# Residual and norm around a feed-forward network, token tile by token tile, and a modulation moved into a convolution

## The chip, the cores and the metric

The kernel runs on one core of a Trainium2 chip. The metric is the device time of one execution in microseconds (us). The core's engines are named as in the profile: PE (TensorE, matmuls and transposes), PEld (its weight loads), DVE (VectorE), ACT (ScalarE), POOL (GpSimd), SP (SyncE, which issues the loads).

## The reference, cut to what matters

256 tokens of width 1024 go through two layers and then a second block. Layer 0 mixes by an mLSTM and an attention, layer 1 by a convolution; each layer has a feed-forward part, dense in layer 0, a mixture of experts in layer 1. The change touches what stands around the dense one and in front of the convolution:

```python
def rmsnorm(x, g):
    xf = x.astype(F32)
    y = xf * lax.rsqrt(jnp.mean(xf * xf, axis=-1, keepdims=True) + EPS)
    return (y * g.astype(F32)).astype(x.dtype)

def adaln(cond, w, b):
    return jax.nn.silu(cond) @ w + b

def modulate(x, g, shift, scale):
    return rmsnorm(x, g) * (1 + scale) + shift

def even_layer(...):
    sh_m, sc_m, gt_m, sh_f, sc_f, gt_f = jnp.split(adaln(c, mod_w, mod_b)[:, None, :], 6, axis=-1)
...
    mix = jnp.concatenate([h_m, h_d], axis=-1) @ w_out
    x = x + gt_m * rmsnorm(mix, mix_post_g)
    y = swiglu(modulate(x, ffn_pre_g, sh_f, sc_f), ffn_w1, ffn_w3, ffn_w2)
    return x + gt_f * rmsnorm(y, ffn_post_g)

def odd_layer(...):
    sh_m, sc_m, gt_m, sh_f, sc_f, gt_f = jnp.split(adaln(c, mod_w, mod_b)[:, None, :], 6, axis=-1)
    u = modulate(x, mix_pre_g, sh_m, sc_m)
    a, g = jnp.split(u @ pw1_w + pw1_b, 2, axis=-1)
    h = a * jax.nn.sigmoid(g)
    h = depthwise_conv(h, dw_w) + dw_b
    h = jax.nn.silu(layernorm(h, ln_g, ln_b))
    y = h @ pw2_w + pw2_b
    x = x + gt_m * rmsnorm(y, mix_post_g)
...
```

`adaln` is the modulation: a vector times a 1024 x 6144 matrix. Layer 1's second and third group of 2048 columns (gate of the convolution, shift, scale and gate of the experts) are not needed before the end of the convolution.

## The kernel before, in words

The 256 tokens lie as two token tiles of 128 partitions; `X` is 128 x 2 x 1024. Matrix products are made of three products of rounded halves: `wsplit` (L247) makes of each loaded weight a high half on ACT (L257) and the rest on DVE (L258), and `mm3` issues the products (L192 to L194). The activations are split as well, into a high tile (`fuTh`, `cuTh`) and a low one (`fuTl`, `cuTl`).

Around the change the program runs so. `w_out_steps` gives the product with `w_out` in four PSUM banks (`o`, two tiles by two halves of 512 columns). `resid` (L499) takes the squares' sums of all four on ACT (`rms_rstd`, L320), makes the gated products `yg` on DVE meanwhile (L506), one root for both tiles (`rsqrt`, L286: a shift guess and three steps, each step two instructions for each column), and adds into `X` (L511). `norm_T` (L490) takes the squares of `X`, a second root, `xn` (L497), and `to_T` (L341) transposes `xn` on PE (`transpose4`, L336) and takes it out of PSUM in pieces of 128 x 256, scaled and shifted: ACT the high half (L357), DVE an unrounded copy `room` (L359) and the rest (L360). This first boundary ends with the first product of the feed-forward network, `ffn0` (L946): eleven blocks of 256 columns, in each `w1` and `w3` by `gemm_T` (`gT` is the product's bank) and then `w2` into four banks `y`. After it the same `resid` and `norm_T` make the second boundary, and the convolution `conv1` (L999) begins: 64 steps of its first matrix `pw1`, between which a depthwise convolution runs chunk by chunk, on DVE or, by shifted copies (`sh` L1044, `shs` L1047, `dw` L1053), on PE, from a padded tile `hpad` (L1024). The order of the instructions on each engine is set when the program is built, by a scheduler over the whole program; pools of PSUM banks and of slots for loads limit it.

`mod_stream` (L433) makes the modulation of a group in eight ticks: a load of 1 MB, four matmuls of 32 columns by 512 (L447; 8 records of the trace a tick), then at the eighth the bias (a DMA, L453, and an addition, L455) and a transpose into columns. In `ffn0` one tick of layer 1's groups 1 and 2 is called behind each of `w1` and `w3` (`tick=1`). `fill` draws steps of work that waits for nothing here (the memory's keys, `mem_k`, of the second block). `gate_rows` (L476) broadcasts a row of the modulation by POOL (`row_bcast`, L469) and multiplies on DVE.

Of the kernel before, what the change touches and what calls it, by code (L numbers as in the profile page):

```python
# [20 lines left out]
D = 1024  # L21
# [12 lines left out]
FILL = (3, 5, 99, 0, 8)  # L34
BEHIND = (2, 1, 4, 2)
# [122 lines left out]
class Net:  # L158
# [278 lines left out]
    def mod_stream(self, todo):  # L437


        nc, t = self.nc, self.t  # L440
        for layer, g, dst, then in todo:
            w = t[f"l{layer}_mod_w"].rearrange("(k p) n -> p k n", p=128)
            p = self.bank("mod", self.mtag)
            for k in range(KC):
                x = self.raw(w[:, k:k + 1, g * 2048:(g + 1) * 2048], 1, 2048)
                for j in range(4):
                    nc.tensor.matmul(p[32 * j:32 * j + 32, :], self.cs[:, k, :], x[:, 0, j * 512:(j + 1) * 512],  # L447
                                     start=(k == 0), stop=(k == KC - 1), tile_position=(0, 32 * j))
                if k < KC - 1:
                    yield  # L450
            b = t[f"l{layer}_mod_b"][g * 2048:(g + 1) * 2048].rearrange("(j n) -> j n", j=4)
            for r in range(2):
                nc.gpsimd.dma_start(self.modb[r:128:32, :], b)  # L453
            mrow = dst()
            nc.vector.tensor_tensor(mrow, p, self.modb, OP.add)  # L455
# [57 lines left out]

    def halved(self, x):
        return [[x[:, tt, j * 512:(j + 1) * 512] for j in range(2)] for tt in range(2)]

    def w_out_steps(self, w, mixT, half=1, bias=None):
# [4 lines left out]
        ps = [[self.bank(f"o{tt}{j}", "g") for j in range(2)] for tt in range(2)]  # L522
# [79 lines left out]
    def layer0(self):  # L602
# [3 lines left out]
        with ExitStack() as es:  # L606
# [318 lines left out]
            self.tick(99)  # L925
            w_out = self.w_out_steps(t["l0_w_out"], mixT, 0)
# [5 lines left out]
            self.resid(ys, gp, self.halved(lp0.tile([128, 2, D], F32, tag="E", name="yg", bufs=2)))  # L932
# [13 lines left out]
    def ffn0(self, gpf, m1rows):  # L946
        nc, t, tc = self.nc, self.t, self.tc
        with tc.tile_pool(name="f0", bufs=1) as fp:
            self.mods1(m1rows, fp, (1, 2))
            uT, uTp = zip(*[self.take([128, KC, 256], F32R, "fuT" + n) for n in "hl"])  # L950
            xnp = self.ring.popleft()
            self.norm_T(self.X, uT[0], uT[1], slice(0, 256), self.scale_cols(0, "fpre0", 0, 3, 4, "a_f0"), xnp)
# [3 lines left out]
            while f0 < FF:  # L956
# [11 lines left out]
                self.gemm_T(t["l0_ffn_w1"], f0, uT, 256, gate, n, "b", tick=1)  # L968
                self.gemm_T(t["l0_ffn_w3"], f0, uT, 256, up, n, "b", tick=1)
                for k2 in range(0, nb, 2):  # L970
                    kk = f0 // 128 + k2
                    w2 = self.wsplit(self.raw(w2v[:, kk:kk + 2, :], 2, D))
                    for k in range(2):
                        hi, lo = w2[k]
                        for tt in range(2):
                            ts = slice(tt * 128, (tt + 1) * 128)
                            for j in range(2):
                                js = slice(j * 512, (j + 1) * 512)
                                self.mm3(yp[tt][j], (hT[0][:, k2 + k, ts], hT[1][:, k2 + k, ts]),
                                         (hi[:, js], lo[:, js]), kk + k == 0, kk + k == FF // 128 - 1)  # L980
# [18 lines left out]
    def conv1(self, mrow):  # L999
        nc, t, tc = self.nc, self.t, self.tc  # L1000
        with tc.tile_pool(name="l1", bufs=1) as lp:
            self.mtag = "b"
            if "l0" not in self.part:
                self.mods1(mrow, lp, (0, 1, 2))
                self.tick(99)
            uT, uTp = zip(*[self.take([128, KC, 256], F32R, "cuT" + n) for n in "hl"])
            self.norm_T(self.X, uT[0], uT[1], slice(0, 256), self.scale_cols(1, "pre1", 0, 0, 1, "a_1"), lp, "sq", fill=FILL[4])
# [59 lines left out]

            for q in range(4):
# [77 lines left out]
    def moe_rows(self, mrow, sp):  # L1146
# [4 lines left out]
        sh = sp.tile([128, D], F32, name="fsh")  # L1151
        for j in range(2):
            sl = slice(j * 512, (j + 1) * 512)
            self.row_bcast(mrow[1], 2 + j, sh[:, sl])
            nc.vector.scalar_tensor_tensor(g[:, sl], self.row_bcast(mrow[2], j), 1.0, g[:, sl], op0=OP.add, op1=OP.mult)
        return g, sh
# [857 lines left out]
    def run(self):  # L2014
        nc, t, tc = self.nc, self.t, self.tc
        part = self.part
        with ExitStack() as es:
# [29 lines left out]
            with tc.tile_pool(name="l1r", bufs=1) as rp:  # L2047
# [12 lines left out]
                self.banks = {"g": 4, "b": 4}  # L2060
# [48 lines left out]
```

## Time and profile before

| | us |
|---|---|
| runs before, median of 3 | 2104.03 (2102.4 to 2105.26) |
| the profiled execution | 2107.45 |
| span of that execution in the profile | 2105.6 |
| PE busy in the span | 1954.2 (93%) |
| DVE busy | 825.5 (39%) |
| ACT busy | 574.1 (27%) |
| POOL busy | 85.8 (4%) |

The profiled execution is 3.4 us above the median; 1.85 us of it lie outside the span. [...] All times of the rows below count from the start of the span. The span covers everything; the change touches some 370 us of it, from 323 us, where the last product with `w_out` ends, to about 691 us, where the layer norm behind the convolution runs.

### The profile page before, as it was taken

Reading aid. Unit: us, or ns where it says so; the run is one execution under the profiler, and the core shown is the slowest. Engines: PE = TensorE matmul, PEld = TensorE weight load, DVE = VectorE, ACT = ScalarE, POOL = GpSimd, SP = SyncE. Lnnn points to the kernel's source line nnn. Section 1 sums busy time; section 2 is a strip of 40 time slices with the busy share of each in tenths; the row PEclk is TensorE's granted clock in tenths of the full one; section 3 lists DMA queues with packets and bytes.
Section 4 is the critical chain, followed back from the end, with each engine's and each line's share of the span. In section 5 each row is a group of like instructions: output and inputs, shape, how many; then the busy total and the mean of one; then the engine's idle time right before and its main releaser. Section 6 shows DMA issues by size and latency. Waiting matters only on the chain. (4 is left out here: it accounts for less than half of the span.)

```text
span 2105.6 us, 32429 instructions
## 1 busy us (share of the span) xinstructions
PE 1954.2 (93%) x13291; PEld 1094.8 (52%) x13291; DVE 825.5 (39%) x1721; ACT 574.1 (27%) x977; POOL 85.8 (4%) x121
## 2 busy tenths in 40 slices
PE   5999897999899899999999999998999998989996
PEld 2777665889777633333333333337733336943442
DVE  4465476444687620012101210117632225662223
ACT  3453254344433510011101101015321213421121
POOL 1010100000130000000000000002000001000000
PEclk9999898999999899999999999999999999999998
DMA  7534557875432489999999999994699998579995
GB/s 300 170 111 140 201 180 259 264 264 178 146 103 100 152 348 412 410 411 410 412 411 410 412 411 413 410 373 154 228 416 421 408 390 310 165 315 422 421 382 235
DMA packets 168659, 635.60 MB, mean 302 GB/s; under 512 B 11969, under 2 KB 57153, under 8 KB 126513
## 3 DMA queue, kind: packets, MB, share of 16 engines
q1 hardware_dynamic: 166128, 631.80, 77.8%
q8 instruction: 110, 1.80, 0.4%
q0 software_dynamic: 2080, 1.04, 0.2%
q10 hardware_dynamic: 288, 0.52, 0.1%
q14 instruction: 53, 0.43, 0.1%
HBM read 632.25 MB, written 1.05 MB: 301 GB/s over the span
## 5 line engine op out<-in xcount | busy, mean ns | idle before, releaser
L1290 PE MATMUL up<-raw,xg 128*32 128x512 f32 (+3 forms) x3456 | 393.7, 563 | 5.8 <-DMA raw<-in_l_moe_w 5.8
L258 DVE TENSOR_TENSOR wh<-raw,wh 128x1024 fp32r<-128x1024 f32 x178 | 216.9, 1224 | 192.2 <-ACT wh L257 191.7
L1290 PEld LDWEIGHTS up<-raw,xg 128*32 128x32 f32 (+1 forms) x3456 | 131.3, 114 | 253.1 <-issue 235.5
L257 ACT ACTIVATE wh<-raw 128x1024 fp32r<-128x1024 f32 x178 | 187.1, 1060 | 245.8 <-PE gT L194 87.3
L1835 PE MATMUL up<-raw,xg 128*64 128x512 f32 (+1 forms) x1088 | 211.1, 595 | 0.0
L1340 PE MATMUL y<-raw,hT 128*32 128x512 f32 (+1 forms) x1584 | 197.6, 600 | 5.0 <-DMA raw<-in_l_moe_w 5.0
L1304 DVE TENSOR_TENSOR h<-up,h 64x512 f32<-64x512 f32 (+5 forms) x63 | 40.8, 647 | 371.0 <-ACT h L1302 370.3
L1302 ACT ACTIVATE h<-up 64x512 f32<-64x512 f32 (+5 forms) x63 | 35.1, 556 | 376.9 <-PE up L1290 376.3
L1861 PE MATMUL y<-raw,hT 128*64 128x512 f32 (+1 forms) x576 | 130.6, 597 | 3.0 <-DMA raw<-in_w_down 1.8
L1835 PEld LDWEIGHTS up<-raw,xg 128*64 128x64 f32 (+1 forms) x1088 | 64.6, 127 | 123.5 <-issue 119.8
L1340 PEld LDWEIGHTS y<-raw,hT 128*32 128x32 f32 (+1 forms) x1584 | 57.2, 114 | 136.9 <-issue 118.4
L192 PE MATMUL gT<-fuTh,wh 128*128 128x256 f32 x352 | 101.0, 287 | 0.0
L193 PE MATMUL gT<-fuTl,wh 128*128 128x256 f32 x352 | 99.5, 283 | 0.0
L194 PE MATMUL gT<-fuTh,wh 128*128 128x256 f32 x352 | 99.5, 283 | 0.0
L1841 DVE TENSOR_TENSOR h<-up,h 64x512 f32<-64x512 f32 x28 | 29.6, 1056 | 154.7 <-ACT h L1840 154.5
L447 PE MATMUL mod<-raw,cs 128*32 128x512 f32 x384 | 64.0, 695 | 26.0 <-DMA raw<-in_l_mod_w 26.0
L1861 PEld LDWEIGHTS y<-raw,hT 128*64 128x64 f32 (+1 forms) x576 | 40.4, 124 | 80.6 <-issue 69.6
L192 PEld LDWEIGHTS gT<-fuTh,wh 128*128 128x128 f32 x352 | 67.4, 191 | 12.1 <-issue 10.9
L1840 ACT ACTIVATE h<-up 64x512 f32<-64x512 f32 x28 | 30.0, 1072 | 155.9 <-PE up L1835 155.9
L194 PEld LDWEIGHTS gT<-fuTh,wh 128*128 128x128 f32 x352 | 67.5, 192 | 0.3
L193 PEld LDWEIGHTS gT<-fuTl,wh 128*128 128x128 f32 x352 | 67.4, 192 | 0.2
L1870 DVE SCALAR_TENSOR_TENSOR yl<-y,gsl,yh 128x512 fp32r<-128x512 f32 x28 | 20.9, 746 | 101.4 <-ACT yh L1869 101.4
(589 smaller groups left out, 3125.3 us busy)
## 6 DMA issues: line engine op xcount, KB each, us to landing
raw<-in_l_moe_w SPq DMA_DIRECT2D x216, 1024.0 KB, 18.4
raw<-in_w_gate SPq DMA_DIRECT2D x64, 1024.0 KB, 10.6
raw<-in_w_up SPq DMA_DIRECT2D x64, 1024.0 KB, 9.7
raw<-in_w_down SPq DMA_DIRECT2D x64, 1024.0 KB, 13.0
raw<-in_l_mod_w SPq DMA_DIRECT2D x48, 1024.0 KB, 6.3
raw<-in_l_moe_w SPq DMA_DIRECT2D x64, 768.0 KB, 17.1
raw<-in_l_ffn_w SPq DMA_DIRECT2D x33, 1024.0 KB, 5.5
raw<-in_l_w_in SPq DMA_DIRECT2D x14, 1024.0 KB, 5.4
```

Of the source, the lines that this page charges most:

```text
L192: mm(out, l[0], r[0], start=start, stop=False, skip_group_check=True)
L193: mm(out, l[0], r[1], start=False, stop=False, skip_group_check=True)
L194: mm(out, l[1], r[0], start=False, stop=stop, skip_group_check=True)
L257: nc.scalar.activation(hi, x[:, k:k + s, :], AF.Copy)
L258: nc.vector.tensor_tensor(lo, x[:, k:k + s, :], hi.bitcast(F32), OP.subtract)
L447: nc.tensor.matmul(p[32 * j:32 * j + 32, :], self.cs[:, k, :], x[:, 0, j * 512:(j + 1) * 512], start=(k == 0), stop=(k == KC - 1), tile_po ...
L1290: nc.tensor.matmul(ps[b][c * t:(c + 1) * t, :hn], j.xg[:, k, s:s + t], x[w][:, k - k2, half * hn:(half + 1) * hn], start=(k == 0), stop=(k ...
L1302: nc.scalar.activation(h[a:z, js], ps[b1][o1:o1 + z - a, :hn], AF.Silu)
L1304: nc.vector.tensor_tensor(h[a:z, js], ps[b3][o3:o3 + z - a, :hn], h[a:z, js], OP.mult)
L1340: nc.tensor.matmul(j.y[b][c * t:(c + 1) * t, :], hT[:, k, s:s + t], x[:, k - k2, o * 512:(o + 1) * 512], start=(i == 0 and k == (k % 2 if ...
L1835: nc.tensor.matmul(p[o:o + t, :], xg[:, k, c:c + t], pair[w][:, k - k4, :], start=(k == 0), stop=(k == KC - 1), tile_position=(0, o))
L1861: nc.tensor.matmul(y[o][a:a + n, :], hT[:, q * m + a:q * m + a + n], x[e][:, k, o * 512:(o + 1) * 512], start=(q == 0), stop=(q == 3), til ...
```

## The change

Five things are changed.

1. `resid` and `norm_T` around the feed-forward network give way to `resid_tiles` and `norm_tiles`, which treat tile 0 and then tile 1, in an order of ACT's and DVE's instructions that is the order of the code (`ordered()`) from the first square to `xn`. Each tile has a root of its own, on operands of 128 x 1. The transposed norm leaves PSUM in pieces of 128 x 128 (16 by ACT, 16 by DVE) with four subtractions of 128 x 512, where it was 8 of 128 x 256 each by ACT, by DVE and for the subtraction.
2. In the last block of `ffn0` the products with `w2` are sorted by token tile.
3. Layer 1's groups 1 and 2 of the modulation leave `ffn0` and go into the loop over `pw1`, a tick behind every third step, in a PSUM bank of their own (tag "m"); the bias is loaded into the row itself.
4. All nine calls of `fill` come ahead of the second residual; one was there before, and eight were inside the norm.
5. The rows made of these groups: the gate behind the convolution and the shift of the experts are made behind the third quarter of the loop, the scale and the last gate behind the loop and what is left of the ticks. All were made behind the second quarter.

```diff
+    def resid_tiles(self, y, gp, yg):
...
+        for tt in range(2):
+            for j in range(2):
+                squares(sums[tt], y[tt][j], j)
+                nc.vector.tensor_tensor(yg[tt][j], y[tt][j], gp[:, j * 512:(j + 1) * 512], OP.mult)
+            r = self.rstd_of(sums[tt], D)
+            for j in range(2):
+                nc.vector.scalar_tensor_tensor(X[tt][j], yg[tt][j], r, X[tt][j], op0=OP.mult, op1=OP.add)
+                squares(sums[2 + tt], X[tt][j], j)
+        return sums[2:]
...
+    def norm_tiles(self, x, sums, hi, lo, sc, xn, chain):
+
+        nc = self.nc
+        for tt in range(2):
+            r = self.rstd_of(sums[tt], D)
+            nc.vector.tensor_scalar(xn[:, tt, :], x[:, tt, :], r, None, op0=OP.mult)
+        chain.close()
+        for k0 in (0, 4):
+            for tt in range(2):
+                ts = slice(tt * 128, (tt + 1) * 128)
+                p = self.transpose4([xn[:, tt, (k0 + i) * 128:(k0 + i + 1) * 128] for i in range(4)])
+                v = self.room()
+                for i in range(4):
+                    pv, k = p[:, i * 128:(i + 1) * 128], k0 + i
+                    nc.scalar.activation(hi[:, k, ts], pv, AF.Identity, scale=sc[0][:, k:k + 1], bias=sc[1][:, k:k + 1])
+                    nc.vector.tensor_scalar(v[:, i * 128:(i + 1) * 128], pv, sc[0][:, k:k + 1], sc[1][:, k:k + 1], op0=OP.mult, op1=OP.add)
+                nc.vector.tensor_tensor(lo[:, k0:k0 + 4, ts], v.rearrange("p (k t) -> p k t", k=4), hi[:, k0:k0 + 4, ts].bitcast(F32), OP.subtract)
...
-            self.mods1(m1rows, fp, (1, 2))
...
-                self.gemm_T(t["l0_ffn_w1"], f0, uT, 256, gate, n, "b", tick=1)
-                self.gemm_T(t["l0_ffn_w3"], f0, uT, 256, up, n, "b", tick=1)
+                self.gemm_T(t["l0_ffn_w1"], f0, uT, 256, gate, n, "b")
+                self.gemm_T(t["l0_ffn_w3"], f0, uT, 256, up, n, "b")
...
+                    order = [(k, tt, j) for k in range(2) for tt in range(2) for j in range(2)]
+                    if f0 + n == FF:
+                        order.sort(key=lambda x: x[1])
...
-            self.tick(99)
             self.ring.extend(uTp)
             self.filler = self.fillers()
-            self.fill(1)
-            self.resid(yp, gpf, self.halved(self.take([128, 2, D], F32, "yg", xnp)[0]))
+            self.fill(1 + FILL[4])
...
+            self.mods1(mrow, (1, 2))
...
+            step = 0
             for q in range(4):
                 for c0, ev in ((0, ev_a), (1024, ev_g)):
                     for _ in self.steps_T(t["l1_conv_pw1_w"], c0 + q * 256, uT, 256, lambda i, p: ev(q * 2 + i, p), 256):
                         behind(BEHIND[0], BEHIND[1])
-                if q == 1:
+                        step += 1
+                        if step % MODS == 0:
+                            self.tick(1)
+                if q == 2:
                     gp = lp.tile([128, D], F32, name="gp1")
                     self.gate_rows(mrow[1], 0, "mpost1", gp)
-                    gpf = self.cp2.tile([128, D], F32, tag="gpf", name="gpf1")
-                    self.gate_rows(mrow[2], 2, "fpost1", gpf)
-                    fsc, fsh = self.moe_rows(mrow, lp)
+                    fsh = self.shift_rows(mrow, lp)
+            self.tick(99)
+            gpf = self.cp2.tile([128, D], F32, tag="gpf", name="gpf1")
+            fsc = self.scale_rows(mrow, lp)
+            self.gate_rows(mrow[2], 2, "fpost1", gpf)
...
-                self.banks = {"g": 4, "b": 4}
+                self.banks = {"g": 3, "b": 4, "m": 1}
```

ACT in the first boundary, before. `junk` is a square's output that nothing reads (its sum is what counts), `o` the product with `w_out`: numbers 2569 and 2570 are tile 0, 2571 and 2572 tile 1; `wh` is the high half of a weight, `fuTh` a piece of the transposed norm.

```order
L320 ACTIVATE junk,ss<-o_2569 128x512
L320 ACTIVATE junk,ss<-o_2570 128x512
L320 ACTIVATE junk,ss<-o_2571 128x512
L320 ACTIVATE junk,ss<-o_2572 128x512
L320 ACTIVATE junk,ss<-X 128x512 x3
L257 ACTIVATE wh<-raw 128x1024
L320 ACTIVATE junk,ss<-X 128x512
L257 ACTIVATE wh<-raw 128x1024 x3
L357 ACTIVATE fuTh<-tp,MC_92,a_f_2828 128x256 x3
```

The four squares of both tiles stand together, ahead of those of `X`.

ACT there after the change (2571 and 2572 are now tile 0, 2573 and 2574 tile 1):

```order
L528 ACTIVATE junk,ss<-o_2571 128x512
L528 ACTIVATE junk,ss<-o_2572 128x512
L528 ACTIVATE junk,ss<-X 128x512 x2
L528 ACTIVATE junk,ss<-o_2573 128x512
L528 ACTIVATE junk,ss<-o_2574 128x512
L528 ACTIVATE junk,ss<-X 128x512
L258 ACTIVATE wh<-raw 128x1024
L528 ACTIVATE junk,ss<-X 128x512
L258 ACTIVATE wh<-raw 128x1024 x4
L560 ACTIVATE fuTh<-tp,MC_92,a_f_2569 128x128 x16
```

Tile 1's squares have moved behind the two of tile 0's `X`, and the pieces of the norm are twice as many and half as wide.

DVE at the same place, before: the gated products of both tiles, then the start of the one root.

```order
L506 TENSOR_TENSOR yg<-o_2569,gp_113 128x512
L506 TENSOR_TENSOR yg<-o_2570,gp_113 128x512
L506 TENSOR_TENSOR yg<-o_2571,gp_113 128x512
L506 TENSOR_TENSOR yg<-o_2572,gp_113 128x512
L328 TENSOR_TENSOR rv_2730<-ss 128x2
L329 TENSOR_SCALAR rv<-rv_2730 128x2
L294 TENSOR_SCALAR rsk<-rv 128x2
```

All four products stand ahead of a root on operands of 128 x 2.

DVE there after the change, from the end of tile 0's root on:

```order
L303 SCALAR_TENSOR_TENSOR rsa<-rsy,rsh 128x1
L308 SCALAR_TENSOR_TENSOR rsy<-rsa,rsy 128x1
L535 SCALAR_TENSOR_TENSOR X<-yg,rsy,X 128x512 x2
L532 TENSOR_TENSOR yg<-o_2573,gp_113 128x512
L532 TENSOR_TENSOR yg<-o_2574,gp_113 128x512
L542 TENSOR_TENSOR ss<-ss 128x1
L543 TENSOR_SCALAR ss<-ss 128x1
L295 TENSOR_SCALAR rsk<-ss 128x1
```

Tile 1's gated products stand behind tile 0's root and its `X`, and a root of their own (on 128 x 1) follows them.

PE between the end of the product with `w_out` and the start of the network, before:

```order
L194 MATMUL o_2572<-wh,mixTl 128x512
L447 MATMUL mod<-raw,cs 32x512 x4
L336 MATMUL tp<-cst,xn 128x128 x12
L447 MATMUL mod<-raw,cs 32x512 x8
L336 MATMUL tp<-cst,xn 128x128 x4
L447 MATMUL mod<-raw,cs 32x512
L192 MATMUL gT<-fuTh,wh 128x256
L193 MATMUL gT<-fuTl,wh 128x256
```

Three rows of modulation stand between `o` and `gT`.

PE there after the change:

```order
L195 MATMUL o_2574<-wh,mixTl 128x512
L337 MATMUL tp<-cst,xn 128x128 x16
L193 MATMUL gT<-fuTh,wh 128x256
L194 MATMUL gT<-fuTl,wh 128x256
L195 MATMUL gT<-fuTh,wh 128x256
```

The modulation's matmuls are gone from between the transposes.

## Rows read from the trace of the kernel before

**Rows 1.** Busy by stretch: start:end, length, PE, PEld, DVE, ACT, POOL, granted clock, DMA share, GB/s.

```profile
323.90:346.20 22.30, 9.25 (x42) 3.67 (x42) 18.94 (x55) 12.38 (x24) 3.31 (x8) 0.62 0.92 308
346.20:544.60 198.40, 198.37 (x1408) 175.56 (x1408) 93.69 (x112) 80.89 (x110) 1.10 (x2) 1.00 0.66 222
544.60:576.80 32.20, 23.59 (x155) 21.19 (x153) 27.77 (x65) 16.63 (x37) 5.54 (x6) 0.95 0.65 205
576.80:691.30 114.50, 109.82 (x974) 81.48 (x974) 96.36 (x187) 44.53 (x73) 20.60 (x25) 0.97 0.31 100
```

**Rows 2.** The same table for line 447 (modulation) alone: PE, PEld, clock, DMA.

```profile
323.90:346.20 22.30, 5.96 (x26) 0.97 (x26) 0.62 0.92 308
346.20:544.60 198.40, 13.85 (x103) 2.04 (x102) 1.00 0.66 222
```

**Rows 3.** PE's timeline in the first boundary: start, length, work [idle before <-releaser].

```profile
335.59 1.94 PE L447 MATMUL mod<-raw,cs 128*32 128x512 f32 x8 [11.69 <-DMA raw<-in_l_mod_w]
...
344.61 0.63 PE L336 MATMUL tp<-cst,xn 128*128 128x128 f32 x4 [0.49 <-DVE room L359]
...
346.24 0.36 PE L192 MATMUL gT<-fuTh,wh 128*128 128x256 f32 x1
```

**Rows 4.** PE's timeline at one tick inside the network.

```profile
387.56 1.07 PE L447 MATMUL mod<-raw,cs 128*32 128x512 f32 x8
388.55 0.38 PE L192 MATMUL gT<-fuTh,wh 128*128 128x256 f32 x1
```

**Rows 5.** DVE's timeline in the first boundary.

```profile
323.28 2.85 DVE L506 TENSOR_TENSOR yg<-o,gp 128x512 f32<-128x512 f32 x4 [1.54 <-ACT junk L320]
...
326.05 0.15 DVE L328 TENSOR_TENSOR rv<-ss 128x2 f32<-128x2 f32 x1
...
326.24 0.17 DVE L329 TENSOR_SCALAR rv<-rv 128x2 f32<-128x2 f32 x1
...
326.71 0.35 DVE L302 SCALAR_TENSOR_TENSOR rsa<-rsk,rsh 128x1 f32<-128x1 f32 x2
...
326.98 0.27 DVE L307 SCALAR_TENSOR_TENSOR rsy<-rsa,rsk 128x1 f32<-128x1 f32 x2
...
328.08 2.73 DVE L511 SCALAR_TENSOR_TENSOR X<-yg,rsy,X 128x512 f32<-128x512 f32 x4
...
335.44 1.22 DVE L258 TENSOR_TENSOR wh<-raw,wh 128x1024 fp32r<-128x1024 f32 x1
...
337.55 1.41 DVE L497 TENSOR_SCALAR xn<-X,rsy 128x1024 f32<-128x1024 f32 x2
...
340.55 0.54 DVE L359 TENSOR_SCALAR room<-tp,a_f,MC 128x256 f32<-128x256 f32 x1
```

**Rows 6.** ACT's timeline in the first boundary: the squares.

```profile
322.56 0.60 ACT L320 ACTIVATE junk<-o 128x512 bf16<-128x512 f32 x1 [2.08 <-PE o L194]
...
324.72 0.60 ACT L320 ACTIVATE junk<-o 128x512 bf16<-128x512 f32 x1
```

**Rows 7.** Busy time in three stretches at half the granted clock.

```profile
326.30:343.30 17.00, 6.84 (x32) 3.12 (x36) 13.76 (x44) 9.91 (x17) 1.66 (x3) 0.50 0.96 338
558.40:561.80 3.40, 3.40 (x16) 3.40 (x17) 2.57 (x5) 0.47 (x1) 0.62 (x1) 0.50 1.10 347
612.98:619.80 6.82, 6.30 (x39) 2.73 (x39) 6.82 (x17) 0.87 (x2) 3.30 (x2) 0.50 0.40 148
```

**Rows 8.** ACT's timeline in the second boundary: the split of a late weight.

```profile
561.33 1.06 ACT L257 ACTIVATE wh<-raw 128x1024 fp32r<-128x1024 f32 x1 [5.87 <-DMA raw<-in_l_conv_pw_w]
```

**Rows 9.** PE's timeline in the second boundary: mem_k's first product, the convolution's.

```profile
558.40 0.55 PE L192 MATMUL gT<-memT,wh 128*128 128x256 f32 x1 [5.07 <-DVE rv L328]
...
576.87 0.39 PE L193 MATMUL gT<-cuTl,wh 128*128 128x256 f32 x1 [0.54 <-DVE cuTl L360]
```

**Rows 10.** Waits of PE in the convolution: us in total, times, longest.

```profile
PE sh L1044 <- DVE hpad L1024: 4.2, 2, 4.0
```

**Rows 11.** Busy time in the convolution's loop over pw1.

```profile
576.80:653.70 76.90, 72.38 (x671) 56.34 (x672) 67.40 (x127) 30.01 (x46) 20.11 (x24) 0.96 0.30 97
```

More of the change, by code (lines that the diff above doesn't have):

```diff
@@ L34 @@
 FILL = (3, 5, 99, 0, 8)
+MODS = 3
 BEHIND = (2, 1, 4, 2)
@@ L512, in resid, with squares, rstd_of @@
         return last
+    def resid_tiles(self, y, gp, yg):
+        nc = self.nc
+        X = self.halved(self.X)
+        sums = self.smp.tile([128, 4, 4], F32, tag="sst", name="ss", bufs=1)
+        sums = [sums[:, q, :] for q in range(4)]
+        def squares(s, x, j):
+            junk = self.wkp.tile([128, 512], BF16, tag="junk", name="junk")
+            nc.scalar.activation(junk, x, AF.Square, accum_out=s[:, j:j + 1])
+        for tt in range(2):
[7 more added lines that the diff above has]
+        return sums[2:]
+    def rstd_of(self, ss, n):
+        nc = self.nc
+        s1, v = ss[:, 2:3], ss[:, 3:4]
+        nc.vector.tensor_tensor(s1, ss[:, 0:1], ss[:, 1:2], OP.add)
+        nc.vector.tensor_scalar(v, s1, 1.0 / n, EPS, op0=OP.mult, op1=OP.add)
+        return self.rsqrt(v)
+    def norm_tiles(self, x, sums, hi, lo, sc, xn, chain):
+        nc = self.nc
+        for tt in range(2):
[12 more added lines that the diff above has]
+                nc.vector.tensor_tensor(lo[:, k0:k0 + 4, ts], v.rearrange("p (k t) -> p k t", k=4), hi[:, k0:k0 + 4, ts].bitcast(F32), OP.subtract)
     def halved(self, x):
@@ L521, in w_out_steps @@
         v = w.rearrange("(k p) n -> p k n", p=128)
-        ps = [[self.bank(f"o{tt}{j}", "g") for j in range(2)] for tt in range(2)]
+        tags = ["g"] * self.banks["g"] + ["m"]
+        ps = [[self.bank(f"o{tt}{j}", tags[2 * tt + j]) for j in range(2)] for tt in range(2)]
         def part(k, tt, j, wt):
@@ L931, in layer0 @@
                 ys[tt][j] = p
-            self.resid(ys, gp, self.halved(lp0.tile([128, 2, D], F32, tag="E", name="yg", bufs=2)))
+            self.chain = ExitStack()
+            self.chain.enter_context(self.ordered())
+            self.sums = self.resid_tiles(ys, gp, self.halved(lp0.tile([128, 2, D], F32, tag="E", name="yg", bufs=2)))
         return gpf
@@ L948, in ffn0 @@
         with tc.tile_pool(name="f0", bufs=1) as fp:
[L949 removed]
             uT, uTp = zip(*[self.take([128, KC, 256], F32R, "fuT" + n) for n in "hl"])
             xnp = self.ring.popleft()
[L952 removed]
+            self.norm_tiles(self.X, self.sums, uT[0], uT[1], (self.af0, self.MC[0][:, 0, 24:32]),
+                            xnp.tile([128, 2, D], F32, tag="raw", name="xn"), self.chain)
             yp = [[self.bank(f"y{i}{j}", "g") for j in range(2)] for i in range(2)]
@@ L972, in ffn0, with mods1 @@
                     w2 = self.wsplit(self.raw(w2v[:, kk:kk + 2, :], 2, D))
-                    for k in range(2):
+                    order = [(k, tt, j) for k in range(2) for tt in range(2) for j in range(2)]
+                    if f0 + n == FF:
+                        order.sort(key=lambda x: x[1])
+                    for k, tt, j in order:
                         hi, lo = w2[k]
[L975 to L980, printed above, removed]
+                        ts, js = slice(tt * 128, (tt + 1) * 128), slice(j * 512, (j + 1) * 512)
+                        self.mm3(yp[tt][j], (hT[0][:, k2 + k, ts], hT[1][:, k2 + k, ts]),
+                                 (hi[:, js], lo[:, js]), kk + k == 0, kk + k == FF // 128 - 1)
                 f0 += n
-            self.tick(99)
             self.ring.extend(uTp)
             self.filler = self.fillers()
-            self.fill(1)
-            self.resid(yp, gpf, self.halved(self.take([128, 2, D], F32, "yg", xnp)[0]))
+            self.fill(1 + FILL[4])
+            self.a1 = self.scale_cols(1, "pre1", 0, 0, 1, "a_1")[0]
+            self.chain = ExitStack()
+            self.chain.enter_context(self.ordered())
+            self.sums = self.resid_tiles(yp, gpf, self.halved(self.take([128, 2, D], F32, "yg", xnp)[0]))
             self.ring.append(xnp)
-    def mods1(self, rows, pool, groups):
-        self.modb = pool.tile([128, 512], F32, name="modb1")
-        self.nc.gpsimd.memset(self.modb, 0.0)
+    def mods1(self, rows, groups):
+        self.modb = None
         self.mods = self.mod_stream([(1, g, lambda g=g: rows[g], None) for g in groups])
@@ L1144, in conv1, with shift_rows, scale_rows @@
         return gpf
-    def moe_rows(self, mrow, sp):
+    def shift_rows(self, mrow, sp):
+        sh = sp.tile([128, D], F32, name="fsh")
+        for j in range(2):
+            self.row_bcast(mrow[1], 2 + j, sh[:, j * 512:(j + 1) * 512])
+        return sh
+    def scale_rows(self, mrow, sp):
         nc = self.nc
```

24 lines of the change are left out of this document (15 added, 9 removed).

## The prediction

> **What bounds the kernel now.** I read the table by stretches first [rows 1], because the change touches four stretches only and the share of the whole span says nothing about one of them. In the feed-forward network (346.2 to 544.6) PE is busy 198.37 of 198.40 us: every microsecond of PE work there is a microsecond of time. In the residual and norm ahead of it (323.9 to 346.2, from here "the first boundary") PE has 9.25 us of work in 22.30; in the one behind it (544.6 to 576.8, "the second") 23.59 of 32.20, and at its start that is still the network's last products. There DVE and ACT, which make squares, roots, products and the transposed halves, set the end. In the convolution PE has 109.82 of 114.50 and DVE 96.36: PE first, DVE close.
>
> So the place of the modulation matters. Its matmuls are busy 13.85 us inside the network and 5.96 us inside the first boundary [rows 2]. The latter are free: between them PE sits idle 11.69 us for a DMA, and the first product of the network starts at 346.24 when the transposed norm is there [rows 3], not when the modulation is done. The former are paid: one tick (8 records) stands between two network products and takes 0.99 us until the next starts [rows 4].
>
> **The change, part by part.**
>
> *The network.* 103 records are 12.9 ticks; at 1.0 us that is 12.9. The two transposes of a finished group go too; I estimate 0.35 us each from the 0.63 us that four transposes with a wait take [rows 3]. Together −13.6. ACT and DVE were busy 80.89 and 93.69 us there [rows 1], so PE stays the bound and nothing covers this gain away.
>
> *The first boundary.* The list of DVE shows that the first product now stands behind all small work of both tiles. I add up DVE from the same start, 323.28 [rows 5]. Prices: a gated product yg 0.7 (2.85 for 4), an X update 0.7 (2.73 for 4), xn 0.7, a split 1.22, all [rows 5]. A root on one 128x1 column: dependent small steps start 0.19 us apart (326.05, 326.24) [rows 5]; a root is 9 dependent starts with one side step, 1.75. Before, one root served both tiles in 2.03 (326.05 to 328.08), because two columns alternate; a boundary now pays 4 roots, 7.0, where it paid 4.06. A 128x128 piece has no row: the 128x256 one takes 0.54 [rows 5], so it lies between 0.27 (half) and 0.54 (all fixed cost); I take the middle, 0.41. The lo subtraction of 512 elements I take as 0.7, like the X update of the same width.
>
> The order of ACT adds a wait. Tile 1's squares now stand behind tile 0's X squares. A square is followed by the next 0.72 us later (322.56, and 324.72 for the fourth) [rows 6]. Tile 0's X updates end at about 327.8, the two X squares at 328.9, the first square of tile 1 at 329.7; yg of tile 1, which stands behind it, has DVE idle 1.9 us. Everything behind on DVE (a root, X, splits, rooms) waits too, and the PE behind those.
>
> The sum until the lo half of both tiles for the first columns: yg 2.8, roots 7.0, X 2.8, wait 1.9, five splits 6.1, xn 1.4, eleven pieces 4.5, two lo 1.4, in all 27.9. That ends at 351.2, where the network ran from 346.3: +4.9. The pieces on ACT (16 now) run beside this. [...] By that row I add 1.7 us (half of 3.4) for a start at half clock, which the ticks had paid before. First boundary **+6.6**; with pieces at 0.27 and no clock loss +3.4, with pieces at 0.54 and more splits ahead +9.
>
> [...]
>
> *The second boundary.* Squares and yg of tile 0 start earlier, since the last w2 block is sorted, but two weight splits stand in the middle of tile 0's root on DVE, and ACT can make them only when a weight has landed: 561.33 in the trace [rows 8]. That row is the floor of the rest. From the DVE split at 562.4: two splits 2.45, the rest of the root 0.8, X 1.4, the same wait for tile 1's squares 1.6, yg 1.4, root 1.75, X 1.4, two roots 3.5, xn 1.4, eleven pieces 4.5, two lo 1.4, two more splits 2.45: 586.5, where the convolution's products run without a gap from 576.87 [rows 9]: +9.6. With 1.7 for the clock **+11.3**. Low bound +4 (pieces 0.27, the weight landing 3 us sooner because no modulation load stands ahead of it in the network), high bound +12.5. In this gap PE finds 21 modulation matmuls before and just behind the first product, 5.25 ticks that cost nothing. The mem_k steps that are drawn ahead (from 558.40 before [rows 9]) fill PE as before; they can't shorten a chain on DVE.
>
> *The convolution.* Of 16 ticks 10.75 are left, 10.75 us, with two transposes of a group 0.7: +11.4. PE waits there 4.2 us for hpad from DVE [rows 10], and runs the 6.82 us behind that wait at clock 0.50 [rows 7], which costs 3.2 of its 6.30 busy. With ticks between, DVE gets that much ahead, and both go: −7.4. The gates' rows move behind tick(99) to the loop's end, where POOL broadcasts them for DVE; I put +2 on it, between 0 (hidden under the last convolution chunks) and 4 (the size of the hpad wait, the nearest row). Convolution **+6.0**. The own PSUM bank and the bias loaded into the row cost nothing while PE works; without that cover, a DMA and an addition per group lie in the open, twice, inside the high bound.
>
> Sum: −13.6 + 6.6 + 11.3 + 6.0 = **+10.3**. The profiled execution took 2107.45, so the changed one would take 2117.8; the median of the runs, 2104.03, is 3.4 below, and the forecast made on it is **2114**. Some 4 us, 0.2%, is about what a measurement can tell from no change.
>
> **Rivals.**
> *Faster, at about 2100: small instructions are cheap.* Two alternating columns start about 0.135 us apart (326.71 to 326.98 for two [rows 5]), so a step might cost 0.12 once it is not bound to its forerunner; then eight roots lose 8 x 6 x 0.07 = 3.4, pieces at 0.27 lose 3.1, and gaps so short would keep the clock, 3.4, and the +2 of the gates hides as well. Sum +10.3 − 11.9 = −1.6; if yg of tile 1 doesn't wait either (3.5), −5; I put it at −4. Place: DVE in both boundaries; it decides where both together grow by less than 7.6 us. Against it: the steps of a single column depend on each other, and rows show 0.19. For it: my bounds.
> *The same, about 2105: the convolution swallows the ticks.* DVE has 67.40 and PE 72.38 us in the 76.9 us from 576.8 [rows 11]. If the chain from DVE to PE paces it, the ticks only fill waits and keep the clock up, and the stretch stays as long as it was: +10.3 − 6.0 = +4.3, and with pieces at 0.27 +1.2. The low bounds of both boundaries alone do as much (−13.6 + 3.4 + 4 + 6.0 = −0.2). Against it: PE idles 4.5 of these 76.9 us only, and DVE keeps its work.
> *Slower, about 2125: loads.* 16 more 1 MB loads go through the convolution's raw slots, and a tick on PE ahead of its load holds every product behind it. In the first boundary PE stood 11.69 us for such a load [rows 3]. At 1 us on each of 11 ticks, 11 more than the forecast. Against it: DMA share is 0.31 there [rows 1].
>
> **How the numbers follow.** The forecast has 0.5, with its own range from 2108 (the convolution unchanged, +4.3) to 2120 (the high bounds of both boundaries and of the gates, +15.9); faster 0.23; the same 0.2; loads 0.07, as slower as the forecast. Range 2098 to 2122: it leaves out the far half of the faster case and most of the loads'. Faster by over 0.2%: 0.23; within 0.2%: 0.2; slower: 0.57.
>
> **What the profile after would show.** Right: no mod matmul in the network and its stretch near 185 us; the first product about 28 us after the first yg; DVE idle before tile 1's yg for ACT's square, 1.6 to 1.9 us in each boundary; 128x128 pieces near 0.41; clock 0.50 at the first network products; convolution some 6 us longer without the hpad wait. Wrong: boundaries of the old length, pieces at 0.27, or a convolution that takes all ticks for nothing, each of which is one of the rivals.

## The result, and the profile after

The changed kernel takes 2126.7 us (median of five runs, 2118.03 to 2129.41); the kernel before took 2105.26 in five runs beside it. The ratio is 1.0091, interval 1.0076 to 1.0106: about 19 us slower (the two medians are 21.4 apart). The forecast was 2114, slower by 10, with a range up to 2122. The sign is right, the size is half of what came, and the time lies outside the range.

The profiled execution (2128.05 us, span 2126.1) is 20.6 us longer in its span than the one before. To compare by stage I cut both traces at the same events of PE: the end of the product with `w_out`, the network's first product with a low half, the end of its last `w2` product, the convolution's first product with a low half, the end of the last `pw1` product, the first sum of the layer norm (`lnm`). All lengths are differences of these times, and differences are taken before rounding.

| us | first boundary | network | second boundary | pw1 loop | loop's tail |
|---|---|---|---|---|---|
| before | 22.5 | 206.2 | 24.2 | 76.9 | 16.7 |
| after | 27.9 | 192.9 | 35.3 | 87.6 | 25.8 |
| difference | +5.4 | −13.3 | +11.1 | +10.8 | +9.1 |
| forecast | +6.6 with the clock's 1.7 | −13.6 | +11.3 | +6.0 for both | |

These five make +23.0; 1.3 come ahead of the cut (there the two programs are nearly the same), and 3.7 are given back behind it. So the network and both boundaries came near the forecast; the convolution, loop and tail, came at +19.8 in place of +6.0. That is more than the whole miss; the 3.7 behind the cut took some of it back.

The busy times by stretch of the changed kernel (first boundary, network, second boundary, loop, tail, and the network's first 6.4 us), columns as in [rows 1]:

```profile
325.20:352.40 27.20, 3.92 (x17) 3.14 (x16) 22.52 (x68) 14.47 (x31) 4.81 (x11) 0.55 0.76 254
352.40:546.00 193.60, 193.44 (x1334) 180.93 (x1335) 101.30 (x123) 87.15 (x121) 0.00 (x0) 0.98 0.48 153
546.00:581.30 35.30, 25.34 (x161) 16.06 (x159) 27.48 (x73) 15.16 (x34) 4.71 (x5) 0.85 0.69 248
581.30:669.00 87.70, 85.96 (x766) 59.45 (x766) 69.47 (x120) 28.81 (x45) 15.86 (x20) 0.98 0.71 240
669.00:694.80 25.80, 20.07 (x226) 12.38 (x225) 14.52 (x29) 5.49 (x10) 4.65 (x7) 0.87 0.25 83
352.40:358.80 6.40, 6.24 (x27) 5.95 (x28) 3.78 (x8) 1.76 (x5) 0.00 (x0) 0.50 0.00 1
```

Of the kernel before, cut at the same events, second boundary, loop and tail:

```profile
552.70:576.90 24.20, 16.56 (x121) 15.55 (x119) 20.11 (x54) 11.49 (x27) 5.54 (x6) 0.93 0.69 224
576.90:653.70 76.80, 72.35 (x671) 56.31 (x672) 67.38 (x126) 29.91 (x46) 20.11 (x24) 0.96 0.30 97
653.70:670.50 16.80, 16.64 (x219) 9.80 (x218) 14.29 (x28) 4.33 (x9) 0.48 (x1) 1.00 0.37 126
```

In loop and tail PE was busy 72.35 + 16.64 = 88.99 us before and 85.96 + 20.07 = 106.03 after: 17.0 us more busy time (some of it only longer, since the tail's clock fell from 1.00 to 0.87), and 2.9 us more idle time. The last row of the first block is the start at half clock: 6.4 us at 0.50, with PE busy 6.24. Products of 128x256 start 0.213 us apart there (353.95 to 358.01) and 0.120 apart behind it (358.96 to 360.88, clock 1.00). I estimate the cost at half of the 6.24, some 3.1, where I took 1.7, half of the 3.40 us at 0.50 in [rows 7].

The modulation's matmuls (line 448 now) in the second boundary and in the loop:

```profile
546.00:581.30 35.30, 9.94 (x42) 1.57 (x42) 0.85 0.69 248
581.30:669.00 87.70, 13.78 (x87) 2.38 (x86) 0.98 0.71 240
```

42 records, 5.25 ticks, found a place in the second boundary, as forecast; 87 records (one lies on the cut and counts twice), 10.75 ticks, stand in the loop and take 13.78 us there, 1.27 each where I took 1.0 from [rows 4]. A whole tick takes no longer there than in the network (1.04 to 1.07 us long, 1.07 in [rows 4]); but three of the ticks come in two parts, of 2 and 6 records (the first of them with its 2 still in the second boundary), and either part takes about as long as a whole tick, 1.03 to 1.06 us in the loop. One of the three, on PE's timeline:

```profile
619.08 1.04 PE L448 MATMUL mod<-raw,cs 128*32 128x512 f32 x2
...
623.80 1.03 PE L448 MATMUL mod<-raw,cs 128*32 128x512 f32 x6
```

DVE's timeline in the first boundary, to be read beside [rows 5]:

```profile
324.60 1.41 DVE L532 TENSOR_TENSOR yg<-o,gp 128x512 f32<-128x512 f32 x2 [1.55 <-ACT junk L528]
325.92 0.15 DVE L542 TENSOR_TENSOR ss<-ss 128x1 f32<-128x1 f32 x1
...
327.89 1.41 DVE L535 SCALAR_TENSOR_TENSOR X<-yg,rsy,X 128x512 f32<-128x512 f32 x2
330.96 1.41 DVE L532 TENSOR_TENSOR yg<-o,gp 128x512 f32<-128x512 f32 x2 [1.66 <-ACT junk L528]
...
346.16 0.75 DVE L551 TENSOR_SCALAR xn<-X,rsy 128x1024 f32<-128x1024 f32 x1
...
348.61 0.41 DVE L561 TENSOR_SCALAR room<-tp,a_f,MC 128x128 f32<-128x128 f32 x1 [0.66 <-ACT fuTh L560]
...
352.40 0.69 DVE L562 TENSOR_TENSOR fuTl<-room,fuTh 128x512 fp32r<-128x512 f32 x1
```

A root takes 325.92 to 327.89, 1.97 us (forecast 1.75); tile 1's product `yg` stands 1.66 us for ACT's square (forecast 1.9); a 128x128 piece takes 0.41 and less, as taken. The network's first product on PE:

```profile
352.42 0.58 PE L193 MATMUL gT<-fuTh,wh 128*128 128x256 f32 x1 [2.63 <-DVE room L561]
```

My list of DVE ended with the low half of both tiles, 27.9 us behind the first `yg`; it is done at 353.1, 28.5 us behind, and the first product starts 27.8 behind. Half the width takes three quarters of the time: a 128x128 piece 0.41 us, a 128x256 one 0.54 [rows 5].

Now the convolution. Waits of PE and of DVE there (waited for: us in total, times, longest), and DVE's and PE's timelines at the loop's end:

```profile
PE sh L1103 <- DVE hpad L1083: 6.1, 2, 5.7
DVE gpf L487 <- POOL room L479: 5.4, 1, 5.4
```

```profile
674.75 0.69 DVE L487 TENSOR_TENSOR gpf<-room,gpf 128x512 f32<-128x512 f32 x1 [5.43 <-POOL room L479]
675.36 0.48 DVE L1091 SCALAR_TENSOR_TENSOR cv<-hpad,dwt,cv 128x256 f32<-128x256 f32 x1
675.75 0.42 DVE L1083 TENSOR_TENSOR hpad<-cv,sg 128x256 f32<-128x256 f32 x1
```

```profile
676.32 3.75 PE L1103 MATMUL sh<-hpad,cst 128*32 128x284 f32 x32 [5.71 <-DVE hpad L1083]
```

PE waits 5.71 us for `hpad`. The `hpad` product was not late for want of DVE's speed: it stands two instructions behind the product `gpf`, which waits 5.43 us for POOL's broadcast of a modulation row. The same wait stands in the kernel before, earlier in the loop:

```profile
602.47 0.69 DVE L482 TENSOR_TENSOR gpf<-room,gpf 128x512 f32<-128x512 f32 x1 [3.85 <-POOL room L474]
```

Those 3.85 us lay behind PE's wait of 4.2 in [rows 10], as kernel 4 below bears out. I read the last link of that chain (DVE) and didn't ask what DVE waited for.

### The profile page after: what moved, and what is told of

It is laid out like the page before. It is cut to its first block, busy times and chain, and to the rows that moved or that the text cites. A ratio compares the mean times of both kernels' runs of the same rounds, so it can differ in the third digit from the quotient of the medians.

```text
span 2126.1 us, 32464 instructions
## 1 busy us (share of the span) xinstructions
PE 1957.5 (92%) x13291; PEld 1100.9 (52%) x13291; DVE 837.7 (39%) x1745; ACT 579.4 (27%) x993; POOL 85.9 (4%) x122
## 3 DMA queue, kind: packets, MB, share of 16 engines
q0 software_dynamic: 2080, 1.04, 0.2%
## 5 line engine op out<-in xcount | busy, mean ns | idle before, releaser
L448 PE MATMUL mod<-raw,cs 128*32 128x512 f32 x384 | 67.0, 708 | 21.4 <-DMA raw<-in_l_mod_w 17.4
## 6 DMA issues: line engine op xcount, KB each, us to landing
raw<-in_w_gate SPq DMA_DIRECT2D x64, 1024.0 KB, 11.1
raw<-in_w_down SPq DMA_DIRECT2D x64, 1024.0 KB, 13.3
```

## The experiments

The ratios are to the kernel before on the same chip. Where none stands, the stretches of the trace count, not the time. The stretches of all kernels:

| us | first boundary | network | second boundary | pw1 loop | tail | ratio to before |
|---|---|---|---|---|---|---|
| before | 22.5 | 206.2 | 24.2 | 76.9 | 16.7 | 1 |
| after | 27.9 | 192.9 | 35.3 | 87.6 | 25.8 | 1.0091 (1.0076 to 1.0106) |
| 1 change, gate late | 27.9 | 192.5 | 33.9 | 89.4 | 17.8 | 1.0057 (1.0035 to 1.0080) |
| 2 tile order alone | 27.0 | 205.8 | 34.2 | 78.1 | 17.9 | 1.0060 (1.0037 to 1.0082) |
| 3 move alone | 20.3 | 192.4 | 23.9 | 89.9 | 24.4 | 1.0012 (0.9999 to 1.0024) |
| 4 before, gates late | 22.5 | 206.1 | 23.5 | 73.1 | 18.1 | 0.9973 (0.9959 to 0.9987) |
| 5 change, squares first | 26.1 | 191.6 | 31.2 | 87.8 | 26.8 | – |
| 6 change, old pieces | 26.5 | 191.8 | 28.0 | 95.3 | 26.4 | – |
| 7 move alone, gate late | 19.5 | 193.6 | 23.7 | 90.1 | 21.8 | 1.0025 (1.0011 to 1.0038) |
| 8 group 2 moved, gates late | 22.5 | 200.2 | 24.0 | 78.9 | 18.3 | 0.9992 (0.9981 to 1.0003) |
| 9 change, one root | 21.5 | 192.5 | 28.6 | 88.0 | 21.9 | – |
| 10 change with 1, 5 and 6 | 24.7 | 192.2 | 26.1 | 94.0 | 18.8 | 1.0062 (1.0045 to 1.0079) |
| 11 change, ticks early | 27.9 | 192.6 | 33.1 | 107.7 | 16.8 | – |
| 12 move alone, all late | 19.7 | 193.5 | 23.9 | 89.9 | 17.6 | 1.0000 (0.9986 to 1.0014) |

**1. The gate out of the way.**

```diff
-            self.gate_rows(mrow[2], 2, "fpost1", gpf)
             while behind(BEHIND[2], BEHIND[3]):
                 self.fill(FILL[3])
...
             self.ring.append(cvp)
+            self.gate_rows(mrow[2], 2, "fpost1", gpf)
```

> The changed kernel, with the last gate (gpf) made behind the layer norm instead of ahead of the last convolution chunks; nothing else. Theory: in the changed kernel DVE waits 5.4 us for POOL's broadcast of this gate, with the last two hpad products queued behind it, PE waits 5.7 us for hpad and then runs some 3.7 us at half clock. With the gate out of the way both go: 7 to 8 us less than the changed kernel, some 12 to 13 us above the kernel before. Rival: ticks and products fill PE, the wait only shows slack, and the last chunks' chain takes as long anyway: within 2 us of the changed kernel.

PE's waits in loop and tail:

```profile
PE gT L195 <- DVE wh L259: 1.3, 1, 1.3
PE sh L1103 <- DVE hpad L1083: 0.5, 2, 0.3
```

The wait for `hpad` is 0.5 in place of 6.1, the tail falls from 25.8 to 17.8, loop and tail together by 6.2; the ratio falls from 1.0091 to 1.0057, some 7 us as expected, though the two intervals still touch. The theory holds.

**2 and 3. The two halves of the change.** Kernel 2 puts the ticks back into the network (`tick=1`, `tick(99)`) and the gates behind the loop's second quarter; kernel 3 puts `resid` and `norm_T` back and leaves the rest of the move.

> The tile order alone: residual, norm, w2's order and the fillers as in the change, but layer 1's modulation stays in the network (a tick behind each w1 and w3) and the gates and PSUM banks of the convolution stay as before. Theory: the first boundary is 5 us longer, the second 11, the network and the convolution are as long as before: 16 us above the kernel before. Rival: the boundaries grew because of what the moved ticks and loads do there (PE and the load queue); with the ticks at home they grow by less than 5 us together.

> The move of the modulation alone: ticks in the convolution, gates as in the change, but residual and norm as before. Theory: the network 13 to 15 us shorter, both boundaries as long as before, the convolution 17 to 20 us longer (11 ticks on a busy PE, and the gate's wait): 3 to 7 us above the kernel before. Rival (the prediction's): the ticks take away the hpad wait and its half clock, so the convolution is only 6 us longer: 5 to 8 us below the kernel before.

The tile order alone costs +4.5 and +10.1 in the boundaries and nothing in the network; at 1.0060 it is 12.6 us slower (I had 16; 1.6 are given back behind). The move alone is 2.5 us slower, a little under the 3 to 7 that I expected, with an interval that touches no change (0.9999 to 1.0024): −13.9 in the network, +13.1 and +7.6 in loop and tail, and −2.2 in the first boundary. That last one I had missed: without ticks and their loads the first boundary is 20.3 long, so the 5.96 us of modulation there were not free, and measured from there the tile order costs 7.6. The trace of the kernel before had it, in a row that [rows 3] leaves out; the last modulation there ends at 346.21, and the network's first product starts at 346.24 without a wait:

```profile
345.16 1.05 PE L447 MATMUL mod<-raw,cs 128*32 128x512 f32 x2
```

**4. The kernel before, with the gates late.** The edit of 1 on the kernel before, with the experts' scale moved to the same place (`moe_rows` in two halves).

> The kernel before, with the scale and the last gate made behind the layer norm; nothing else. Theory: DVE's wait of 3.8 us for POOL goes, and with it PE's wait of 4.0 us for hpad and the 6.8 us at half clock behind it (3.2): 5 to 7 us below the kernel before. Rival: the gate only took the blame, the chunks on DVE set the end of the loop: within 2 us of the kernel before.

Loop and tail, and PE's wait for `hpad`:

```profile
580.70:653.80 73.10, 71.98 (x671) 57.26 (x672) 65.13 (x123) 29.84 (x46) 9.89 (x12) 0.98 0.31 102
653.80:671.90 18.10, 18.10 (x225) 11.36 (x224) 14.48 (x28) 5.50 (x10) 0.71 (x2) 1.00 0.54 175
```

```profile
PE sh L1044 <- DVE hpad L1024: 1.1, 2, 0.9
```

The wait is 1.1 in place of 4.2 [rows 10], the loop 3.7 us shorter at clock 0.98 where it was 0.96 [rows 11], the tail 1.3 longer, the second boundary 0.7 shorter; 2102.55 us against 2108.61 beside it, ratio 0.9973, 5.7 us as expected. This is the one kernel here that is faster than the kernel before. How much of the 5.7 is the gates' is less sure: its profile is the slowest of its ten runs (2108.18), and the five stretches together are only 3.2 us shorter there. The last gates can be made so late because nothing needs them sooner: the scale is done at 677.7 and first read at 727.9.

**5, 6 and 9. What makes the boundaries long.** Kernel 5 issues the four squares of `y` first; kernel 6 takes the norm out of PSUM by `to_T`, as before; kernel 9 has one root on 128x2 in `resid_tiles` and one in `norm_tiles`.

```diff
         for tt in range(2):
             for j in range(2):
                 squares(sums[tt], y[tt][j], j)
+        for tt in range(2):
+            for j in range(2):
                 nc.vector.tensor_tensor(yg[tt][j], y[tt][j], gp[:, j * 512:(j + 1) * 512], OP.mult)
```

> The changed kernel, with the squares of both tiles of y on ACT ahead of everything else of the residual; nothing else. Theory: DVE's wait of 1.66 us for tile 1's square ahead of its gated product goes, in both boundaries, and all behind it moves up: each boundary 1.5 to 2 us shorter than in the changed kernel (27.9 and 35.3). Rival: the wait only takes the place of later waits for weights and for ACT's pieces: under 0.5 us each.

> The changed kernel, with the transposed norm taken out of PSUM as before, in pieces of 128x256 that hold both tiles, 8 by ACT, 8 by DVE and 8 subtractions; roots and residual stay tile by tile. Theory: the first product needs one piece instead of eight pieces and two subtractions of 512, so 3 to 5 us of each boundary's growth (5.4 and 11.1) go. Rival: the four roots and the wait for the squares are the growth, the pieces run beside other work: under 1 us each.

> The changed kernel, with one root on 128x2 for both tiles in the residual and one in the norm (so the squares of y also stand together again); the pieces of 128x128, the moved modulation and the gates stay. Theory: of each boundary's growth the roots are 2.9 us and the wait for the squares 1.7, so the first boundary is 4 to 5 us shorter than the changed kernel's 27.9 and the second 4 to 6 shorter than its 35.3; with the pieces left, neither is back at the length before with no ticks in it (20.3 and 23.9 in the move alone). Rival: the pieces hold everything, and the roots run in the shade of the weight splits: under 2 us each.

The squares are worth 1.9 and 4.1 us (I had 1.5 to 2 for each); the pieces 1.4 and 7.3 (I had 3 to 5); one root with the squares together 6.5 and 6.7 (I had 4 to 5 and 4 to 6). In the first boundary the theory on the pieces fails, and the roots are worth more than I had. In the second the three together are more than its whole growth, so they can't be added. DVE's timeline in the first boundary of kernel 9:

```profile
323.32 2.85 DVE L533 TENSOR_TENSOR yg<-o,gp 128x512 f32<-128x512 f32 x4 [1.55 <-ACT junk L529]
...
328.12 2.73 DVE L537 SCALAR_TENSOR_TENSOR X<-yg,rsy,X 128x512 f32<-128x512 f32 x4
...
335.30 1.41 DVE L561 TENSOR_SCALAR xn<-X,rsy 128x1024 f32<-128x1024 f32 x2
...
338.90 0.73 DVE L571 TENSOR_SCALAR room<-tp,a_f,MC 128x128 f32<-128x128 f32 x2
```

Counted from the first `yg`, the last `xn` is done after 13.4 us, where the changed kernel took 22.3, though the pieces are still 128x128; the first product comes 6.5 sooner, and the rest goes to four weight splits of about 1.2 each, which stand behind the last `xn` here and ahead of it in the changed kernel. In the second boundary only two splits stand behind the last `xn`, and the pieces count. But kernel 6 gives the 7.3 us back in the loop, 95.3 in place of 87.6. PE's waits there, one of ACT's, and ACT's timeline at the longest of PE's:

```profile
PE gT L195 <- DVE wh L259: 6.9, 2, 6.2
PE sh L1094 <- DVE hpad L1074: 5.9, 1, 5.9
```

```profile
ACT wh L258 <- DMA raw<-in_l_conv_pw_w: 23.7, 5, 7.5
```

```profile
608.52 1.06 ACT L258 ACTIVATE wh<-raw 128x1024 fp32r<-128x1024 f32 x1 [5.40 <-DMA raw<-in_l_conv_pw_w]
```

PE stands 6.2 us for one split weight, whose load came late. This is the third rival (loads). My reading is that 16 more loads in the same slots leave no slack once the boundary doesn't hide them; no run here varies the slots. In the changed kernel itself PE waits 1.3 us there for such a weight, and for no load directly.

**7, 8, 10, 11 and 12. Can the move pay?** Kernel 7 is kernel 3 with the gate late, 12 the same with the scale late too; 8 leaves group 1 in the network; 10 joins 1, 5 and 6; 11 has `MODS = 1`.

> The move of the modulation alone (residual and norm as before), with the last gate behind the layer norm. Theory: of the move alone's stretches (network -13.9, first boundary -2.2, loop +13.1, loop's tail +7.6) only the tail falls, by 7: 4 to 6 us below the kernel before. Rival: without the gate's wait the ticks' 16 us on PE stay in the loop and something else holds the tail: within 2 us of the kernel before.

> Residual and norm as before; of the modulation group 1 stays in the network and group 2 goes into the convolution; scale and last gate behind the layer norm. Theory: a tick costs 1.0 us in the network and 1.1 in the convolution's loop, the gates' place is what pays: 5 to 7 us below the kernel before, as with the gates alone. Rival: fewer ticks in the loop leave PE's waits there to hide them for nothing: 9 us below or more.

> The changed kernel with three mendings at once: squares of both tiles first, pieces of 128x256, last gate behind the layer norm. Theory: boundaries near 24 and 25 us, the loop's tail near 18, but the loop longer by the ticks that no longer fit into the second boundary (near 95): 5 to 8 us above the kernel before. Rival: with the mended boundaries the tile order wins back what it cost: within 2 us of the kernel before or below it.

> The changed kernel with a tick behind every step of the loop in place of every third. Theory: what fails is the place of the gate's rows, which come late because the last tick comes late; with all ticks in the first quarter of the loop POOL's chain is done early and the tail is back at 17 to 18 us (25.8 in the changed kernel), while the ticks still cost PE their 1.1 to 1.3 us each, and PE waits for some loads: loop 88 to 94. Rival (loads): sixteen 1 MB loads cannot come so fast, PE waits 10 us or more for them in the loop.

> The move of the modulation alone (residual and norm as before), with both the scale and the last gate behind the layer norm, as in the kernel before with late gates. Theory: DVE's waits for POOL (3.9 and 1.9 us in the tail) go, the tail is at 17 to 18.5; loop and tail together are then 16 to 18 us longer than in the kernel before with late gates (73.1 and 18.1), which is all of the 15 ticks: they are paid in full, none hides in DVE's work; the whole is within 3 us of the kernel before. Rival (the prediction's): with the gates out of the way the ticks do fill PE's waits, and loop and tail are no more than 10 us longer than there.

Kernel 7 failed my expectation (4 to 6 us below; it came 5 above): its tail is 21.8, since DVE still waits 3.9 us for the broadcast of the scale, as it did in kernel 3 (4.3). Kernel 8 is level, where I expected 5 to 7 below: half the ticks moved cost the loop and tail 5.9 us more than kernel 4 and save 5.9 in the network. In kernel 10 the stretches come as expected, with a loop of 94.0, but the whole is 13 us slower than before, where I had 5 to 8. Kernel 11 shows that a gate made early holds DVE as well. Its waits of DVE in the loop:

```profile
DVE gp L487 <- POOL room L479: 9.4, 2, 6.1
DVE gpf L487 <- POOL room L479: 8.8, 1, 8.8
DVE fsc L1225 <- POOL room L479: 6.1, 1, 6.1
```

All rows are ready early, the products stand earlier in DVE's list, and DVE waits 24.3 us for POOL in all. The tail is 16.8, a little under the 17 to 18 that I had, the loop 107.7, where I had 88 to 94: I had moved POOL's chain, and DVE's place in front of it moved with it. The ticks' loads are not cleared by this: in the changed kernel and the one before, POOL's waits for its small DMAs were 2.8 to 4.5 us beside loads, elsewhere 1.1 to 1.8 (last section). Kernel 12 gives the clean price of the ticks, with nothing waiting for POOL in loop and tail but 2.1 and 0.7 us:

```profile
560.00:649.90 89.90, 88.27 (x802) 59.10 (x799) 71.74 (x129) 28.65 (x46) 11.69 (x14) 1.00 0.80 271
649.90:667.50 17.60, 17.58 (x221) 11.89 (x220) 10.54 (x22) 5.37 (x10) 0.67 (x2) 1.00 0.17 61
```

```profile
560.00:649.90 89.90, 17.43 (x122) 3.10 (x118) 1.00 0.80 271
```

107.5 us for loop and tail, 16.3 above kernel 4's 91.2, and PE is busy 105.85 of them. The second block is line 448 alone: 122 records, 15.25 ticks, take 17.43 us. They are paid in full; next to nothing hides. What this kernel saves in the network and the first boundary (12.7 and 2.8 us) it spends here.

## Why the prediction was right in sign and wrong in size

- **The network** (−13.6): right at −13.3, but two parts were off and cancelled. The start at half clock, which the forecast put into the first boundary with 1.7 (from another restart, the 3.40 us of [rows 7]), lasted 6.4 us and costs by my estimate some 3.1, nearly all of it inside the network; without it the saving is about 16. Of the some 2.5 above my sum, 1.0 is a wait of PE at the end of the old network that is gone; the rest I did not take apart. Network and first boundary together were forecast at −7.0 and came at −7.9.
- **The first boundary** (+6.6, of it 1.7 for the clock): right by its sum, +5.4 for the other 4.9. Again two parts were off and cancelled: the ticks in it were not free (−2.2), against what I read into [rows 3], and the roots and the wait behind them weighed more (kernel 9).
- **The second boundary** (+11.3): right by its sum, +11.1, ticks found there 5.25, as said. Its parts are not shown one by one, since kernels 5, 6 and 9 take more off it together than it grew.
- **The convolution** (+6.0): wrong, +19.8. The step that failed is "With ticks between, DVE gets that much ahead, and both go: −7.4". DVE was not short of time; it stood in its queue for POOL, 3.85 us before and 5.43 after. The wait moved with the gate from the loop's middle to its end, with 5.7 us on PE and a slow start behind it (the tail's clock is 0.87, it was 1.00). Kernels 1 and 4 divide the loop and tail: 93.6 us before, 91.2 with the old gates out of the way (kernel 4), 107.2 with the ticks added and the gate out of the way (kernel 1), 113.4 in the changed kernel. So the old wait was worth 2.4 us even where it goes, not 7.4; the ticks, with what else differs between these two kernels, cost 16.0, where I had 11.4; and the gate at its new place costs 6.2, where stands "I put +2 on it, between 0 ... and 4". Of the ticks' excess some 3 are the three ticks in two parts, 13.8 us of matmuls for 10.75.
- **The rivals.** Cheap small instructions: refuted, a root on one column takes 1.97. A convolution that swallows the ticks: refuted by kernel 12. Loads: PE waits for none directly in the changed kernel's convolution (in its second boundary 1.5 us for the loads of two ticks); in kernel 6, where the boundary no longer covers them, it waits for a weight that came late. None of them was the one that came: the wait I thought removed came back in another place.

What stays open: 3.7 us that the changed kernel gives back in the experts' stages and behind, where the programs are nearly the same (in the other kernels that stretch moved by −3.2 to +3.8 without a pattern); why PE's wait for `hpad`, 4.2 us with a half clock behind it, was worth only 2.4 in kernel 4; and why the scheduler takes some ticks apart. I did not try them.

## What to carry to other kernels

When a wait is to go because its engine gets ahead, look up what that engine itself waits for at that moment: the row one link further back (here DVE for POOL, 3.85 us) decides whether more time helps. A product that needs a row which POOL broadcasts late should stand in the queue behind everything that others wait for; moving it behind the last such product was worth some 7 us on the changed kernel and, by the times, 6 on the kernel before, where the whole change lost 19. And work moved from one stage that PE bounds to another can cost there what it saved (in kernel 12 16.3 us for 15.5), so the idle time that is to take it should be shown row by row.

## What the runs showed of the hardware that I had not expected

- A gate is a chain on POOL of four small DMAs and four broadcasts, one after the other. In the changed kernel, POOL's timeline, some of its broadcasts:

```profile
649.30 0.50 POOL L476 DMA_DIRECT2D mod_row<-m1row  x1 [5.65 <-issue]
654.25 0.79 POOL L479 PARTITION_BROADCAST room<-mod_row  x1 [4.45 <-DMA mod_row<-m1row]
...
661.54 0.90 POOL L184 PARTITION_BROADCAST gpf<-row_fpost  x1 [2.77 <-DMA row_fpost<-in_rowv]
...
667.51 1.67 POOL L184 PARTITION_BROADCAST gpf<-row_fpost  x1 [4.29 <-DMA row_fpost<-in_rowv]
...
673.92 0.79 POOL L479 PARTITION_BROADCAST room<-mod_row  x1 [3.96 <-DMA mod_row<-m1row]
```

These are the scale's last two rows and three of the gate's four. From the DMA at 649.30 to the broadcast that frees DVE, at 673.92, pass 24.6 us, 16.6 of them five waits of 1.1 to 4.5 us for DMAs of 2 KB; the broadcasts themselves take 0.8 to 1.7.

- How long POOL waited for such a small DMA went with what else the DMA engines did. Three of these waits as stretches, columns as in [rows 1], the DMA engines' share last but one:

```profile
649.80:654.25 4.45, 4.45 (x40) 2.63 (x40) 3.76 (x9) 1.72 (x4) 0.00 (x1) 1.00 1.04 411
655.83:656.97 1.14, 1.14 (x13) 0.42 (x11) 1.14 (x3) 0.16 (x1) 0.00 (x1) 1.00 0.02 2
669.96:673.92 3.96, 0.64 (x3) 0.19 (x1) 0.00 (x0) 0.53 (x1) 0.00 (x1) 0.86 0.65 249
```

At a share of 0.02 the wait is 1.1 us, at 0.65 and 1.04 it is 4.0 and 4.5; the other two of the five are 2.8 and 4.3 at 0.66 and 0.64. In the kernel before, between 585 and 628, such waits are 1.2 to 1.8 us at a share of 0.02 to 0.06 and 2.8 to 3.9 at 0.44 to 0.77. So the loads of weights and ticks may well make the gate late; no run here makes a gate with the loads held back.

- ACT and DVE took turns on some pieces of the transposed norm. ACT's timeline at the end of the first boundary:

```profile
354.70 0.46 ACT L560 ACTIVATE fuTh<-tp,MC,a_f 128x128 fp32r<-128x128 f32 x1 [0.48 <-DVE room L561]
355.64 0.46 ACT L560 ACTIVATE fuTh<-tp,MC,a_f 128x128 fp32r<-128x128 f32 x1 [0.48 <-DVE room L561]
```

A piece of 0.46 us comes every 0.94 us, each time behind DVE's `room` of 0.41, and DVE's waits in turn 0.53 for ACT's. Of ACT's 16 pieces there six wait for `room`, 5.0 us in all; eight others, from 348.97 on, come one behind the other in 3.54 us. In the trace the six wait for the other engine's semaphore; what the chip would do without, no run here tells.

- The program ahead of the change, nearly the same in all kernels, ended between 319.2 and 328.7 us in the profiles. That is about as wide as the spread of one kernel's runs (2118 to 2129 for the changed one). With one profile of each kernel it is not shown to be the cause, but it is a reason to compare stretches and not spans.
